# Layer 0's products of probabilities with v: fp32 products replaced by split fp32r products with hi and lo of v side by side

## The chip, the core and the metric

The kernel runs on one core of a Trainium2 chip. The metric is the device time of one execution in microseconds, the median of several runs. A core has a matrix engine (TensorE, PE in the profile; its weight loads are PEld), VectorE (DVE), ScalarE (ACT), GpSimd (POOL) and SyncE (SP), which work at the same time, each through its own queue of instructions in a fixed order, and wait for one another by semaphores. SBUF is the memory on the chip with 128 partitions, PSUM the banks in which TensorE's products add up.

## The reference, cut to what matters

Two layers of a trunk run for 128 prompt tokens and 512 latent tokens with 1024 features. Layer 0 has two attention mixers beside each other, whose outputs meet in one output projection; then an MLP; layer 1 has another mixer and MLP, which the change doesn't touch.

```python
q_a, k_a, v_a, q_b, k_b, v_b = parts          # of h @ w_in, heads of 64 features
# mixer A: 8 query heads on 2 key and value heads, 512 + 128 (cached) keys, softmax over all 640
s = jnp.einsum('bqkgd,bskd->bkgqs', qi, k).astype(jnp.float32) * scale
p = jax.nn.softmax(s, axis=-1).astype(v.dtype)
o = jnp.einsum('bkgqs,bskd->bqkgd', p, v)
# mixer B: 8 heads; each query reads 8 x 16 neighbours on the grid, with a bias, and 128 cached keys
s = jnp.concatenate([s_loc.reshape(B, H, GRID_W, n_loc), s_ctx], axis=-1)
p = jax.nn.softmax(s, axis=-1).astype(v.dtype)
o = (jnp.einsum('bhqrw,brqwhd->bqhd', p_loc, vn) + jnp.einsum('bhqp,bphd->bqhd', p_ctx, v_ctx))
```

Prompt tokens read only prompt tokens (128 x 128 per head) in both mixers. The new keys and values of the prompt are outputs too.

## The kernel before

Nearly all products of weights with activations are split: a value x is kept as hi = fp32r(x) and lo = x - hi, both in fp32r (fp32 numbers that TensorE reads with less precision), and three products hi·hi, lo·hi and hi·lo add up in one bank (L245 to L247 for blocks of 128 features and 320 tokens, L463 to L465 for 256 columns token by token). The products of probabilities with v aren't split: both sides are fp32.

Layer 0's attention is `attn_layer`. After the modulation and norm come mixer A's q, k and v, their norms and the rotary step (`ev_kv` puts v's blocks into `va`, feature rows `qaT` hold the queries, `kha` the split keys). Then `pair_a` runs for four pairs of heads. For each head and 128 queries the scores (L691) lie in PSUM, VectorE takes their maximum (L616), ScalarE the exponential with sums (L621), VectorE the sums' reciprocals (L622), GpSimd multiplies (L623). `turned` transposes four blocks of 128 x 128 probabilities into one bank `t` (L631), and one copy brings them to SBUF as `pt`: by VectorE for the odd head of a pair (L634), by ScalarE for the even one (L636). The product with v (L700) takes 64 columns of v as stationary side and 512 queries as moving side, for five key blocks. The two heads of a pair write to the upper and the lower 64 partitions of one bank `o`; five products each add up, and VectorE copies the bank to a tile `oa` (L704). `prompt_block` does the same for the prompt's 128 x 128 (L645 to L658).

Behind the pairs in the program's order stand `pieces`, the projections of mixer B's v (evacuated to `vall` by ScalarE, L710), q and k (`ev_b`, L722 to L743: copy, square, sum over partitions by a product, logarithm and exponential, multiply). The scheduler places them among the heads' instructions, wherever TensorE would wait. Then mixer A's outputs `oa` are split into hi and lo (L235 on ScalarE, L236 on VectorE).

Mixer B's pool of buffers takes the place of mixer A's queries, keys and v (`mid`). The cached keys of all heads come in one load `craw` (L769, on ScalarE's queue), and become `ckb`, hi and lo (L770, L771). `front(h)` is a head's scores (L797 to L801), the bias add (L803) with a bias block from HBM (L781, SyncE's queue), and softmax. Hi and lo of the head's keys `kk` are made by L783 and L784 and sent to the other 64 partitions by a DMA (L786). `back(pr, pss)` does the products with v of two heads side by side in one bank: the 128 cached keys for all 512 queries (L823), then four key blocks for 256 queries each (L833). `put_b` splits the bank straight from PSUM: hi on ScalarE (L813), lo on VectorE (L814). The order of the fronts, prompt blocks and backs is a list: F0 F1 F2 F3 P0 P1 B0 F4 F5 P2 B1 F6 F7 P3 B2 B3. Filling work in mixer B are products of modulation weights (L170).

This whole part stands in one phase that a scheduler orders by a timeline of its own; the order of each engine's instructions is fixed when the program is built. The phase ends with a barrier of all engines (L78).

## Time and profile before

| what | us |
| --- | --- |
| median of 3 runs | 1877.26 |
| the runs | 1877.03, 1877.26, 1878.83 |
| span of the profiled execution, first to last instruction | 1874.1 |
| layer 0's attention with its norm, start to the barrier L78 | 0 to 358 |
| mixer A's heads with mixer B's projections | 95 to 282 |
| mixer B's heads | 282 to 358 |

The profile is of one execution on the one core; its own device time outside the span isn't listed apart. Times in rows are microseconds from the span's start. A window gives how long each engine was busy in a stretch; a group of instructions gives busy time, mean ns of one, and the idle time in front of them with what ended it; a row of a timeline gives start, duration, engine, line, operation, output and inputs. An fp32 product appears as two records. A matmul's record is longer than the distance between two starts, since matmuls are pipelined: costs of TensorE are read from the starts. In a shape such as 128\*64 the second number is that of the stationary columns.

### The profile page before, as it was taken

To read this page: it belongs to the slowest core of one execution; us is meant where nothing else is said; L and a number is where in the kernel's file an instruction comes from. 1 tells how busy PE (TensorE), PEld (TensorE's weight loads), DVE (VectorE), ACT (ScalarE), POOL (GpSimd) and SP (SyncE) were. 2 spreads that over 40 slices of the span, in tenths; PEclk is the share of its full clock that TensorE was granted. 3 is DMA by queue.
4 is the path that set the end of the run, shared out by engine and by line. 5 is a ranking of instruction groups with operands and counts; after the bars stand their busy time and mean duration, and the time that the engine had idled before them with its cause. 6 is when DMAs were issued, how large, how long until landed. Compare 5 with 4: busy or idle time off the path is not lost.

```text
span 1874.1 us, 34901 instructions
## 1 busy us (share of the span) xinstructions
PE 1792.9 (96%) x14416; PEld 1662.4 (89%) x14416; DVE 1120.3 (60%) x2252; ACT 781.6 (42%) x1725; POOL 252.3 (13%) x252
## 2 busy tenths in 40 slices
PE   5899998999999999999989999999999999999999
PEld 4887776698999999999888878888999999999999
DVE  5745348478766666746687877776447434343342
ACT  4535456345223131233655656655635213132230
POOL 1223314211000000001332222222111000000000
PEclk9999999999999999999999999999999999999999
DMA  9201028524454344423223122232132222222221
GB/s 317 77 27 48 25 81 289 181 75 157 138 177 135 136 146 147 158 97 103 72 53 74 48 47 69 48 89 74 49 124 77 82 68 75 83 68 72 87 75 50
DMA packets 174990, 187.21 MB, mean 100 GB/s; under 512 B 48456, under 2 KB 152136, under 8 KB 174832
## 3 DMA queue, kind: packets, MB, share of 16 engines
q1 hardware_dynamic: 170272, 175.05, 29.7%
q0 software_dynamic: 1408, 5.41, 0.9%
q10 hardware_dynamic: 3152, 4.52, 0.7%
q8 instruction: 113, 1.85, 0.4%
q14 instruction: 45, 0.37, 0.1%
HBM read 170.97 MB, written 11.37 MB: 97 GB/s over the span
## 4 chain that ended last, share of the span: by engine, by line
PE 59%; DVE 10%; issue 7%; ACT 3%; DMA 1%; POOL 1%; DVEq 0%; SPq 0%; POOLq 0%; ACTq 0%
PE dn L245 10%; PE dn L246 9%; PE dn L247 9%; PE p L245 8%; PE p L246 8%; PE p L247 8%; DVE t L229 1%; DMA t<-in_w_out_dram 1%; PE p L1265 1%; PE p L1256 1%; PE ob L1258 1%; PE ob L1282 1%; DVE at L1116 1%; PE p L1277 1%; PE s L1046 1%
## 5 line engine op out<-in xcount | busy, mean ns | idle before, releaser
L228 ACT CAST t<-t 128x1024 fp32r<-128x1024 f32 x157 | 164.4, 1048 | 346.3 <-PE p L246 237.8
L245 PE MATMUL dn<-t 128*128 128x320 f32 x936 | 298.7, 319 | 4.1 <-PEq L78 3.1
L246 PE MATMUL dn<-t 128*128 128x320 f32 x936 | 299.3, 320 | 1.3 <-DVE t L395 0.8
L247 PE MATMUL dn<-t 128*128 128x320 f32 x936 | 297.6, 318 | 0.0
L229 DVE TENSOR_TENSOR t<-t 128x1024 fp32r<-128x1024 f32 x157 | 193.4, 1233 | 121.7 <-ACT t L228 121.3
L245 PEld LDWEIGHTS dn<-t 128*128 128x128 f32 x936 | 178.1, 190 | 9.6 <-issue 5.4
L246 PEld LDWEIGHTS dn<-t 128*128 128x128 f32 x936 | 178.0, 190 | 6.0 <-issue 2.5
L247 PEld LDWEIGHTS dn<-t 128*128 128x128 f32 x936 | 178.0, 190 | 3.3 <-issue 2.5
L245 PE MATMUL p<-t 128*128 128x320 f32 x488 | 152.0, 311 | 0.0
L247 PE MATMUL p<-t 128*128 128x320 f32 x488 | 151.6, 311 | 0.0
L246 PE MATMUL p<-t 128*128 128x320 f32 x488 | 151.6, 311 | 0.0
L407 DVE SCALAR_TENSOR_TENSOR x<-p,t,x 128x192 f32<-128x192 f32 (+2 forms) x154 | 53.3, 386 | 143.6 <-PE p L247 143.6
L246 PE MATMUL p<-hl,t 128*128 128x320 f32 x448 | 138.4, 309 | 0.0
L192 DVE SCALAR_TENSOR_TENSOR ma<-t,ma 128x1024 f32<-128x1024 f32 x98 | 123.4, 1280 | 18.7 <-DMA t<-in_mod_w_dram 18.7
L246 PE MATMUL dn<-hl,t 128*128 128x320 f32 x416 | 128.5, 309 | 0.0
L245 PE MATMUL p<-hh,t 128*128 128x320 f32 x392 | 121.1, 309 | 0.0
L247 PE MATMUL p<-hh,t 128*128 128x320 f32 x392 | 121.1, 309 | 0.0
L245 PE MATMUL dn<-hh,t 128*128 128x320 f32 x376 | 116.4, 310 | 0.0
L247 PE MATMUL dn<-hh,t 128*128 128x320 f32 x376 | 116.2, 309 | 0.0
L429 ACT CAST hh<-h 128x320 fp32r<-128x320 f32 x128 | 58.7, 459 | 126.9 <-DVE h L428 126.9
L388 POOL TENSOR_TENSOR nt<-x,rs 128x320 f32<-128x320 f32 x30 | 31.4, 1062 | 566.6 <-ACT rs L308 536.9
L246 PEld LDWEIGHTS p<-t 128*128 128x128 f32 x488 | 92.3, 189 | 0.2
(458 smaller groups left out, 4575.6 us busy)
## 6 DMA issues: line engine op xcount, KB each, us to landing
t<-in_mlp_w_dram SPq DMA_DIRECT2D x64, 1024.0 KB
t<-in_mod_w_dram SPq DMA_DIRECT2D x40, 1024.0 KB, 7.0
t<-in_w_qkv_dram SPq DMA_DIRECT2D x12, 1024.0 KB
t<-in_w_in_dram SPq DMA_DIRECT2D x9, 1024.0 KB, 5.9
w<-in_mod_w_dram SPq DMA_DIRECT2D x4, 2048.0 KB, 16.4
t<-in_w_out_dram SPq DMA_DIRECT2D x8, 1024.0 KB, 5.2
bias<-in_biasx_dram SPq DMA_DIRECT2D x8, 512.0 KB, 6.8
t<-in_w_z_dram SPq DMA_DIRECT2D x4, 1024.0 KB
```

The source lines that it names most:

```text
L192: nc.vector.scalar_tensor_tensor(out=acc[v], in0=wt[:, k], scalar=c, in1=acc[v], op0=ALU.mult, op1=ALU.add)
L228: nc.scalar.copy(hi, raw)
L229: nc.vector.tensor_tensor(out=lo, in0=raw, in1=hi.bitcast(F32), op=ALU.subtract)
L245: self.nc.tensor.matmul(ps, lhsT=hi[:, k, :], rhs=xh[:, ts_], start=(k == 0), stop=False)
L246: self.nc.tensor.matmul(ps, lhsT=hi[:, k, :], rhs=xl[:, ts_], start=False, stop=False)
L247: self.nc.tensor.matmul(ps, lhsT=lo[:, k, :], rhs=xh[:, ts_], start=False, stop=(k == NK - 1))
L388: nc.gpsimd.tensor_tensor(out=t, in0=xt[k][:, c], in1=rs[:, c], op=ALU.mult)
L407: nc.vector.scalar_tensor_tensor(out=xout[:, a:b], in0=ps[:, a - o:b - o], scalar=self.mod_vec(layer, idx, k, v), in1=xin[:, a:b], op0=ALU ...
L429: nc.scalar.copy(hh[:, ts_], h)
L1046: nc.tensor.matmul(pn[32 * g:32 * g + 32, 0:3 * P], lhsT=n.ones[:, 0:32], rhs=sq[g % 2][:, g // 2 * 2 * P:g // 2 * 2 * P + 3 * P], start=T ...
L1116: nc.vector.scalar_tensor_tensor(out=aa[:, d, b0 + b, :], in0=ps[:, b, 0], scalar=bk[:, b0 + b, d:d + 1], in1=ga[d][:, b0 + b, :], op0=ALU ...
L1256: nc.tensor.matmul(p1s[d][:, 0:128], lhsT=K[:, 0, bs], rhs=S[d], start=True, stop=True)
```

## The change

`split_v` keeps v in fp32r as 128 columns for each head: 64 of hi and 64 of lo (`va`, `vall`); every evacuation of v becomes a cast by ScalarE and a subtraction by VectorE, and so do the cached v, which now come by way of a tile `cv`. The prompt's new v for the output is copied apart (`vo`). `turned` makes hi (ScalarE) and lo (VectorE) of each transposed bank, in 2 + 2 buffers in place of 4, for every head. `with_v` is the product: one with all 128 columns (v's hi and lo) and hi of the probabilities, whose output has 128 partitions, and one with the 64 columns of v's hi and lo of the probabilities into the first 64 partitions. `halves` adds the bank's two halves: ScalarE copies the lower one to SBUF, VectorE adds. Each head now has the bank `o` to itself, and the heads of a pair come one after the other in both mixers. Mixer A's result is written over its queries `qaT`, and their split stands ahead of the release of mixer A's pool. Mixer B's result goes to a tile `ob` and is split from there.

```diff
+    def split_v(dst, src):
+        sv = src.rearrange("p (h d) -> p h d", d=HD)
+        nc.scalar.copy(dst[:, :, 0:HD], sv)
+        nc.vector.tensor_tensor(out=dst[:, :, HD:2 * HD], in0=sv, in1=dst[:, :, 0:HD].bitcast(F32), op=ALU.subtract)
...
-        vall = qp.tile([P, 6, HB * HD], F32, name="vall")
+        vall = qp.tile([P, 6, HB, 2 * HD], F32R, name="vall")
-        va = [ap_.tile([P, KVA * HD], F32, name=f"va{blk}") for blk in range(6)]
+        va = [ap_.tile([P, KVA, 2 * HD], F32R, name=f"va{blk}") for blk in range(6)]
...
-            p = n.wsp.tile([P, nb * w], F32, tag=f"p{nb}", name="p", bufs=8 if nb == 1 else 10)
+            p = n.wsp.tile([P, nb * w], F32, tag=f"p{nb}", name="p", bufs=7 if nb == 1 else 10)
...
-            pt = n.wsp.tile([P, 512], F32, tag="pt", name="pt", bufs=4)
-            if j:
-                nc.vector.tensor_copy(pt[:, 0:w], t[:, 0:w])
-            else:
-                nc.scalar.copy(pt[:, 0:w], t[:, 0:w])
-            return pt
+            hi, lo = (n.wsp.tile([P, 512], F32R, tag=f"pt{i}", name="pt", bufs=2)[:, 0:w] for i in range(2))
+            mulsub(hi, lo, t[:, 0:w])
+            return hi, lo
+
+        def with_v(out, v, hi, lo, start, stop):
+            nc.tensor.matmul(out, lhsT=v, rhs=hi, start=start, stop=False, skip_group_check=True)
+            nc.tensor.matmul(out[0:HD], lhsT=v[:, 0:HD], rhs=lo, start=False, stop=stop, skip_group_check=True)
+
+        def halves(dst, o):
+            w = o.shape[1]
+            u = n.wsp.tile([P, 512], F32, tag="oh", name="oh", bufs=1)
+            nc.scalar.copy(u[HD:P, 0:w], o[HD:P])
+            nc.vector.tensor_tensor(out=dst, in0=o[0:HD], in1=u[HD:P, 0:w], op=ALU.add)
...
-                    pts = [turned(j, [pb[:, 0, kb * P:(kb + 1) * P] for pb in pss[j]]) for j in range(2)]
-                    for j in range(2):
-                        nc.tensor.matmul(o[64 * j:64 * j + 64, :], lhsT=vs[kb if kb < 4 else 5], rhs=pts[j], start=(kb == 0), stop=(kb == 4))
+                heads = [qaT[pr][64 * j:64 * j + 64] for j in range(2)]
+                for j in range(2):
+                    o = n.bank("o")
+                    for kb in range(5):
+                        pt = turned([pb[:, 0, kb * P:(kb + 1) * P] for pb in pss[j]])
+                        with_v(o, vs[kb if kb < 4 else 5], *pt, kb == 0, kb == 4)
+                    halves(heads[j][:, 0:TS], o)
...
-                sq = bp.tile([P, T], F32, tag="bsq", name="bsq")
+                sq = bp.tile([P, T], F32, tag="bsq", name="bsq", bufs=1)
...
+        for k, t in enumerate(qaT):
+            n.split_act(k, t)
         mid.close()
-        for k, t in enumerate(oT):
-            n.split_act(k, t)
...
+                oT = out_b(TS, 1)
                 for j in range(2):
-                    nc.tensor.matmul(o[64 * j:64 * j + 64, :], lhsT=val(5, j), rhs=pts[j], start=True, stop=False, skip_group_check=True)
...
+                    o = n.bank("o")
+                    with_v(o, val(5), *turned([pb[:, 256:384] for pb in pss[j]]), True, False)
...
+                            with_v(ov, val(kb), *(x[:, ji * 256:(ji + 1) * 256] for x in pt), False, kb == 3)
+                    halves(oT[64 * j:64 * j + 64], o)
+                split_b(pr, oT, [(0, 384, 64), (384, 448, 0), (448, 512, 448)])
```

Comments are gone from the changed file, so lines move: L691 becomes L707, L803 L817, L769 L783; the helper of hi and lo (before L450, L451) is L445 and L446, and `turned` and `put_b`'s splits now go through it.

How the instructions stand on the queues is shown at three places. The names are the tiles' (`t` is also that of transposes' banks, of weights and of split activations), the last number is the output's shape, and in brackets are the engines or DMA queues that an instruction waits for. First TensorE, around mixer A's first products with v; before:

```order
L700 MATMUL o<-pt,va_536 64x512 [waits Activation_85]
L631 MATMUL t<-t,p 128x128 [waits PE_85]
L631 MATMUL t<-t,p 128x128 x3
L463 MATMUL dn<-t 128x256
L464 MATMUL dn<-t 128x256
L465 MATMUL dn<-t 128x256
L700 MATMUL o<-pt,va_536 64x512 [waits DVE_85]
L631 MATMUL t<-t,p 128x128 [waits PE_85]
L631 MATMUL t<-t,p 128x128 x3
L700 MATMUL o<-pt,va_537 64x512 [waits Activation_85]
L631 MATMUL t<-t,p 128x128 [waits PE_85]
```

and after:

```order
L645 MATMUL o<-pt,va_536 64x512 [waits DVE_85]
L637 MATMUL t<-t,p 128x128 [waits PE_85]
L637 MATMUL t<-t,p 128x128
L644 MATMUL o<-pt,va_537 128x512 [waits Activation_85]
L637 MATMUL t<-t,p 128x128 x2
L465 MATMUL dn<-t 128x256
L466 MATMUL dn<-t 128x256
L645 MATMUL o<-pt,va_537 64x512 [waits DVE_85]
L660 MATMUL t<-kha_544,qs 128x128 [waits PE_85]
```

A product is now two, the second of which waits for VectorE's lo, and other work stands between the two or behind them; transposes for the other head of the pair no longer alternate with these.

Second ScalarE, where mixer B begins: the load of the cached keys and what stands around it (`bx` and `bsq` are the evacuation and norm of a projection of mixer B, `qs` the split queries). Before:

```order
L769 DMA craw<-in_ctxk_dram 128x1024 [waits DVE_85,PE_85]
L450 CAST qs<-qbT_523 64x640 x2
L450 CAST qs<-qbT_524 64x640 x2
L734 ACTIVATE bsq<-t 128x320 [waits PE_85]
L734 ACTIVATE bsq<-dn,t 128x320 [waits PE_85]
L783 CAST t<-kbT_527 64x640 [waits PE_85]
L734 ACTIVATE bsq<-o,t 128x320 [waits PE_85]
L735 ACTIVATE bsq<-bsq 128x640 [waits Activation_85]
L734 ACTIVATE bsq<-dn,t 128x320 [waits PE_85]
L770 CAST ckb_2859<-craw 128x1024 [waits DMAHW2_85]
```

and after:

```order
L749 ACTIVATE bsq<-o,t 128x320 [waits PE_85]
L737 COPY bx<-sc 128x320 [waits PE_85]
L750 ACTIVATE bsq<-bsq 128x640 [waits Activation_85]
L783 DMA craw<-in_ctxk_dram 128x1024 [waits DMAHW0_85,DVE_85]
L445 CAST qs<-qbT_523 64x640 x2
L445 CAST qs<-qbT_524 64x640
L797 CAST kk_3051<-kbT_528 64x640
L445 CAST qs<-qbT_524 64x640
L744 ACTIVATE bsq<-bx 128x640 [waits DVE_85]
L784 CAST ckb_3056<-craw 128x1024 [waits DMAHW0_85]
```

The load waited for TensorE's and VectorE's use of mixer A's buffers, with projections still to come; now it waits for VectorE's splits of mixer A's output and stands behind the evacuation of the last projection.

Third VectorE, at the end of mixer B, up to the barrier. Before:

```order
L229 TENSOR_TENSOR t<-t 128x1024 [waits Activation_85]
L634 COPY pt<-t 128x512 [waits DVE_85,PE_85]
L814 TENSOR_TENSOR t<-o,t 128x384 [waits Activation_85]
L634 COPY pt<-t 128x512 [waits DVE_85,PE_85]
L814 TENSOR_TENSOR t<-o,t 128x64 [waits Activation_85] x2
L634 COPY pt<-t 128x512 [waits DVE_85,PE_85]
L814 TENSOR_TENSOR t<-o,t 128x384 [waits Activation_85]
L814 TENSOR_TENSOR t<-o,t 128x64 [waits Activation_85] x2
```

and after:

```order
L446 TENSOR_TENSOR t<-ob,t 128x384 [waits Activation_85]
L446 TENSOR_TENSOR t<-ob,t 128x64 [waits Activation_85] x2
L446 TENSOR_TENSOR pt<-t,pt 128x512 [waits PE_85,Activation_85]
L446 TENSOR_TENSOR pt<-t,pt 128x512 [waits Activation_85]
L652 TENSOR_TENSOR ob<-o,oh 64x512 [waits DVE_85,Activation_85]
L446 TENSOR_TENSOR pt<-t,pt 128x512 [waits Activation_85]
L446 TENSOR_TENSOR pt<-t,pt 128x512 [waits PE_85,Activation_85]
L652 TENSOR_TENSOR ob<-o,oh 64x512 [waits Activation_85]
L446 TENSOR_TENSOR t<-ob,t 128x384 [waits Activation_85]
L446 TENSOR_TENSOR t<-ob,t 128x64 [waits Activation_85] x2
```

Each bank of transposes passes over VectorE, and each head has an add of its halves (L652) ahead of the split.

## Rows read from the trace of the kernel before

**Rows 1.** The profile page's span, and its section 1.

```profile
span 1874.1 us, 34901 instructions
...
PE 1792.9 (96%) x14416; PEld 1662.4 (89%) x14416; DVE 1120.3 (60%) x2252; ACT 781.6 (42%) x1725; POOL 252.3 (13%) x252
```

**Rows 2.** Windows: busy us by engine (instructions), granted clock, DMA share, GB/s.

```profile
70.00:80.00 10.00, 10.00 (x86) 10.00 (x85) 10.00 (x23) 5.45 (x16) 4.09 (x6) 1.00 0.36 109
95.00:256.00 161.00, 159.80 (x984) 120.77 (x984) 72.62 (x126) 68.06 (x150) 47.20 (x36) 0.99 0.10 30
282.00:300.00 18.00, 12.94 (x132) 9.56 (x131) 16.65 (x31) 13.97 (x40) 6.17 (x8) 1.00 0.91 290
300.00:340.00 40.00, 39.72 (x329) 26.62 (x330) 30.30 (x61) 22.89 (x72) 16.68 (x16) 0.96 0.77 253
282.00:358.00 76.00, 66.81 (x566) 44.45 (x565) 56.53 (x110) 45.50 (x131) 25.74 (x24) 0.98 0.66 217
```

**Rows 3.** Groups by line and shape, 95 to 256 us (mixer A).

```profile
L700 PE MATMUL o<-pt,va 128*64 128x512 f32 x80 | 39.7, 618 | 0.1
...
L634 DVE COPY pt<-t 128x512 f32<-128x512 f32 x20 | 13.8, 691 | 47.2 <-PE t L631 47.1
...
L636 ACT COPY pt<-t 128x512 f32<-128x512 f32 x20 | 11.7, 587 | 33.1 <-PE t L631 33.1
```

**Rows 4.** Timeline of TensorE in mixer A: start us, us, instruction.

```profile
155.56 0.27 PE L631 MATMUL t<-t,p 128*128 128x128 f32 x1
155.76 1.07 PE L700 MATMUL o<-pt,va 128*64 128x512 f32 x2
156.77 0.41 PE L245 MATMUL dn<-t 128*128 128x320 f32 x1
157.02 0.31 PE L246 MATMUL dn<-t 128*128 128x320 f32 x1
157.16 0.31 PE L247 MATMUL dn<-t 128*128 128x320 f32 x1
```

**Rows 5.** Timeline around mixer B's start, all engines; last, the DMA issues.

```profile
255.26 0.36 ACTq L769 DMA_DIRECT2D craw<-in_ctxk_dram  x1
...
255.66 2.98 ACT L450 CAST qs<-qbT 64x640 fp32r<-64x640 f32 x4 [1.85 <-PE o L658]
...
262.13 1.03 ACT L770 CAST ckb<-craw 128x1024 fp32r<-128x1024 f32 x1
...
263.19 1.23 DVE L771 TENSOR_TENSOR ckb<-craw,ckb 128x1024 fp32r<-128x1024 f32 x1 [0.86 <-ACT ckb L770]
...
282.12 0.31 PE L247 MATMUL sc<-t 128*128 128x320 f32 x1
...
282.32 0.74 ACT L735 ACTIVATE bsq<-bsq 128x640 f32<-128x640 f32 x1
...
283.32 0.70 DVE L803 TENSOR_TENSOR sc<-sc,bias 128x512 f32<-128x512 f32 x1
...
craw<-in_ctxk_dram ACTq DMA_DIRECT2D x1, 512.0 KB, 6.5
```

**Rows 6.** Groups by line and shape, 282 to 358 us (mixer B).

```profile
L833 PE MATMUL o<-pt,vall 128*64 128x256 f32 x64 | 11.0, 391 | 0.4 <-ACT pt L636 0.4
...
L823 PE MATMUL o<-pt,vall 128*64 128x512 f32 x16 | 5.4, 618 | 0.0
```

**Rows 7.** Timeline of VectorE and TensorE at the end of mixer B.

```profile
338.38 0.70 DVE L803 TENSOR_TENSOR sc<-sc,bias 128x512 f32<-128x512 f32 x1 [0.20 <-PE sc L801]
...
357.25 0.23 DVE L814 TENSOR_TENSOR t<-o,t 128x64 fp32r<-128x64 f32 x1 [0.28 <-ACT t L813]
...
352.38 1.08 PE L823 MATMUL o<-pt,vall 128*64 128x512 f32 x4
353.29 2.07 PE L833 MATMUL o<-pt,vall 128*64 128x256 f32 x16
358.42 0.38 PE L245 MATMUL dn<-t 128*128 128x320 f32 x1 [3.06 <-PEq L78]
```

More of the change, by code (lines that the diff above doesn't have):

```diff
@@ L440, in attn_layer @@
     I, O = n.i, n.o
[L441 to L446 removed]
+    bps = ExitStack()
     def mulsub(hi, lo, src):
@@ L806, in front, with out_b @@
                 return pbs, q, kk
-            def put_b(pr):
-                def put(ps, pieces):
-                    hi, lo = n.act[8 + 2 * pr:10 + 2 * pr]
-                    for a, b, d in pieces:
-                        c = slice(d, d + b - a)
-                        nc.scalar.copy(hi[:, c], ps[:, a:b])
-                        nc.vector.tensor_tensor(out=lo[:, c], in0=ps[:, a:b], in1=hi[:, c].bitcast(F32), op=ALU.subtract)
-                return put
+            def out_b(w, bufs):
+                return wp.tile([P, w], F32, tag=f"ob{w}", name="ob", bufs=bufs)
```

78 lines of the change are left out of this document (36 added, 42 removed).

## The prediction

> **What bounds the kernel now.** I read the page first, then the windows, then lines, single rows and waits of the stretches that the change touches. The span is 1874.1 us and TensorE is busy for 96% of it [rows 1]. The change lies in layer 0's attention, the first 358 us; the next part starts behind a barrier, at 358.42, where TensorE's idle time is put down to its own sequencer [rows 7]. The instructions behind that barrier stand in the same order as before, so I let those 1516 us stay as they are. What matters is when the barrier is reached.
>
> The windows [rows 2] show four stretches with different limits. At 70 to 80 us (norms and rotary step of mixer A) VectorE is busy for 10.00 of 10 us. From 95 to 256 us (mixer A's heads, with projections as filling) TensorE is busy for 159.80 of 161 us and VectorE for 73: TensorE's own time counts. From 282 to 300 us (mixer B begins) TensorE has 12.94 of 18, VectorE 16.65: VectorE leads. From 300 to 340 us TensorE has 39.72 of 40 and VectorE 30.30: both are well filled. Behind 340 a chain of transposes, copies and products runs out, from the last bias add at 338.38 to the last subtraction at 357.25 [rows 7]. A gain in the second stretch can so be given back in the three others.
>
> **Mixer A, products with v.** A lone product starts at 155.76 and the next work at 156.77: 1.01 us [rows 4]. The 80 records of the 40 products [rows 3] have starts that add up to 37.1 us, 0.93 each, since some follow one another. The first wide product behind takes 0.25 us (156.77 to 157.02), the second 0.15 (157.02 to 157.16) [rows 4]: going from 64 stationary columns back to 128 costs 0.10 in that row. With a somewhat longer last record I take 0.15 for a change of shape. The 40 products cost 37.1 us and 0.14 each for what lies outside, 42.7 us.
>
> Now each is a product of 128 and one of 64 stationary columns, 512 moving columns, fp32r. No row has an fp32r product with 64. The nearest is the fp32r product with 128: 0.15 us for 320 columns [rows 4], 0.23 for 512; a quarter of the fp32 product, as if it were four passes, is 0.23 also. I take 0.22. Going to 64 columns and back costs two changes: 0.22 + 0.22 + 0.30 = 0.74 us, times 40 is 29.6 us, **13.1 us less**. The ends: no cost for a change, 17.6 us and 25 less; the 64-column product at the old 0.93, 58 us and 15 more. I stay at 0.74 since fp32r and the change both have near rows. Four prompt blocks get 16 short products for 8, with changes of shape: 1.7 us more (estimate, 0.2 us a product). So TensorE's time in this stretch falls by 11.4 us.
>
> The Trainium skill, "TensorEngine Tiling (Array Packing)", Theoretical Speedup and Key Properties, says that up to 64 columns leave room for two tiles that work in parallel, up to twice as fast; that speaks against the change. The trace shows it where two heads' products adjoin, in mixer B: four records, two products, in 0.91 us (352.38 to 353.29) [rows 7]. In mixer A 1.01 us for a lone product says that it was hardly used. Had it been, the 40 products would have cost some 24 us, the change would save nothing here, and the time would be about 1900 us.
>
> **What the copies become.** Every transposed block had one copy, 0.59 us on ScalarE or 0.69 on VectorE, 20 each in this stretch [rows 3]. Now each of the 40 has both, one behind the other: 20 more on each engine, 11.7 and 13.8 us. The new sum of the halves adds a copy and an add per head (0.59 and 0.69), the splits of v more short ones. VectorE goes from 73 to about 90 us and ScalarE from 68 to about 87, of some 150: TensorE hides them, if filling stands between a transpose and its product. With two banks for transposes, two buffers each for hi and lo, and one bank for a head's sum, I add 1.5 us of new waits (0 to 4; 40 blocks with 0.1 us each uncovered is 4). The eight copies of mixer A's output go away; they were hidden and bring nothing.
>
> **Ahead of mixer A** VectorE is full [rows 2], and five splits of v's blocks and the cache's come there: six subtractions at 0.3 us (between 0.23 for 64 columns [rows 7] and 0.69 for 512 [rows 3]), **1.8 us more** (0 to 3). So the last projection ends 11.4 - 1.5 - 1.8 = **8.1 us earlier** than 282.12 (4 to 12).
>
> **Mixer B's start.** Before, the load of the cached keys was issued at 255.26 on ScalarE's queue, its cast ran at 262.13 and its subtraction at 263.19, all under the projections; the first bias add came at 283.32, 1.2 us behind the last projection's start at 282.12 [rows 5]. Now this buffer lies where mixer A's queries lie, and these become free only when mixer A's output in them has been split. Those splits write over the projections' input, so they can't end before the last projection. On ScalarE's queue the load now stands behind the copy of the last projection and an exponential of 0.74 us [rows 5]: issued some 1.3 us behind the last projection. It lands 6.5 us later [rows 5]; the casts of queries queued meanwhile (2.98 us for four) lie under that. Then cast 1.03, subtraction 1.23, and about 1 us of scores: the first bias add comes 1.3 + 6.5 + 1.03 + 1.23 + 1 = 11 us behind the last projection, 10 more than before. SyncE's queue has the first bias block behind the splits too, which lands in the same time. What TensorE, VectorE and ScalarE do meanwhile (modulation products, prompt scores, key splits) they did later before; I count 2 us as given back: **8 us more** (5 to 10).
>
> **The rest of mixer B.** VectorE gets 12 more blocks of 512 at 0.69, two or so of 256, eight adds of 512 columns and eight of 128: 8.3 + 0.8 + 5.5 + 2 = some 15 us on top of 56.5 [rows 2]; ScalarE about the same on 45.5. TensorE: two heads' products took 3.0 us in one go (352.38 to 355.36) [rows 7], but the 80 records [rows 6] lie scattered, and with changes of shape and prompt products I count 21.8 us before. Now a head has five pairs: 512 columns 0.44, four of 256 at 0.24, five times 0.30: 2.9 us, eight heads 23.2, prompts about 4: **5 us more** (1.5, without cost for a change less than nothing, to 11). TensorE's 66.8 us become 72, VectorE's 56.5 become 71.5. The stretch is 76 us. If VectorE is filled as at 282 to 300, 93%, it needs 77; at its mean of 74% it needs 96. TensorE alone needs 72. I take the middle, 83%: 86 us, **10 us more** (2 to 20). More than half of that I expect behind the last bias add, where heads that were done side by side come one after the other, each with copy, subtraction, products, copy, add, and the second waits for the first one's bank.
>
> **Sum.** -8.1 + 8 + 10 = +10 us. The profiled span is 1874.1 us, the median of the runs 1877.26; that execution's time outside its span isn't listed, and I take the 3.2 us between them as unchanged. So 1877.3 + 10 = **1887 us**.
>
> **Rivals.**
> 1. *Mixer B takes its new work in its gaps, and mixer A's gain stays.* TensorE is idle for 9 of 76 us there, VectorE for 19, and the wait at the start would be filled with work that came later. Decides if the start and the rest together cost under 4.4 us, since 8.1 are gained: start 3, rest 1, TensorE's gain at its 12 end: 1877 - 12 + 4 = 1869, or 1873 with the middle gain. For it: the row of 282 to 358 leaves room. Against it: VectorE at 93% in the first 18 us, and a tail in which each step waits for the one before.
> 2. *Gain and loss cancel*: gain 8 to 12, start 5, rest 4: 1877 us. It needs both losses at their low ends.
> 3. *The 64-column fp32r product isn't faster than the old one*, so the change doesn't do what it says: 0.93 + 0.22 + 0.30 for each of 40, 58 us; 28 us more than in the sum, and some 15 more in mixer B: about 1925 us. No row has it, but the 128-column row speaks against it.
>
> **How the numbers follow.** Forecast, slower, 1887 us: 0.60. Rival 1: 0.22. Rival 2: 0.15. Rival 3: 0.03. The measurement can tell a change of about 0.2%, 3.75 us: faster 0.22, same 0.15, slower 0.63. Where it is slower, 1881 to 1903 holds most. Over all cases 8 in 10 lie from 1870 (half of rival 1) to 1902 us (mixer B at its upper end, +18, with the other terms in the middle, and rival 3 left out).
>
> **What would show it.** Right: lines of mixer A's two new products with starts about 0.3 us apart and the window's TensorE time some 11 us smaller; the last projection 4 to 12 us earlier; the load of cached keys behind it and the first bias add 8 to 11 us behind it; over 20 us between the last bias add and the barrier. Wrong: if the 64-column product takes over 0.5 us, if the first bias add follows the projections within 4 us, or if mixer B's stretch is not longer than 78 us. Changes behind the barrier would mean that I missed a part.

## The result: 12.5 us slower

The changed kernel takes 1889.8 us (median of 4 runs, 1885.53 to 1891.11) beside 1877.35 us for the kernel before: 1.0058 times as long, 95% interval 1.0042 to 1.0073. The forecast was 1887 us, range 1870 to 1902, slower 0.63.

The page of the changed kernel, its span and its section 1, answers [rows 1]:

```profile
span 1889.4 us, 35114 instructions
...
PE 1786.3 (95%) x14416; PEld 1686.4 (89%) x14416; DVE 1160.7 (61%) x2329; ACT 816.9 (43%) x1798; POOL 250.7 (13%) x252
```

TensorE is busy for 6.6 us less, VectorE for 40 more, ScalarE for 35 more, and the span is 15.3 us longer. The time was thus not lost in TensorE's work. The windows say where. The columns are those of [rows 2]; the borders are the changed kernel's own: norms of mixer A, mixer A, last projection to first bias add, start, middle and end of mixer B.

```profile
70.00:80.00 10.00, 10.00 (x86) 10.00 (x85) 10.00 (x22) 5.68 (x15) 3.96 (x6) 1.00 0.37 111
95.00:267.20 172.20, 163.13 (x1123) 148.95 (x1122) 100.48 (x175) 101.19 (x217) 45.92 (x36) 0.99 0.13 38
267.20:277.50 10.30, 7.25 (x57) 5.09 (x57) 8.45 (x11) 8.21 (x13) 5.15 (x8) 0.83 0.91 303
277.50:300.00 22.50, 15.05 (x113) 10.33 (x116) 12.98 (x24) 10.14 (x31) 4.92 (x7) 0.62 0.89 272
300.00:343.80 43.80, 35.53 (x286) 28.36 (x279) 37.66 (x74) 29.28 (x82) 17.18 (x16) 0.84 0.69 209
343.80:371.20 27.40, 19.51 (x117) 14.26 (x115) 19.81 (x41) 16.95 (x41) 2.93 (x2) 0.94 0.00 1
```

The last projection starts at 267.17 in place of 282.12, **14.95 us earlier**. Behind it mixer B takes 104.1 us (to 371.24, the end of the last subtraction) in place of 75.4 (282.12 to 357.48 [rows 5, 7]), **28.7 us more**. In the second window TensorE is busy for 95% of the time; from 277.5 to 300 it has 15.05 of 22.5 us at a granted clock of 0.62, where [rows 2] have 1.00. The barrier is reached 13.8 us later, and what lies behind it takes 1518.2 us in place of 1516.6.

Mixer B is best cut in three: from the last projection to the third bias add (the second head's first; a head's scores fill both of the tiles `sc`, so the third bias add waits until the first two exponentials have read the first one), from there to the last bias add, and the end behind that. Before, the cuts are 282.12, 289.52, 338.38 and 357.48; now 267.17, 293.00, 343.76 and 371.24. This gives 7.4, 48.9 and 19.1 us before, and 25.8, 50.8 and 27.5 after. **The middle, where most of the new copies are, costs 1.9 us; the start costs 18.4 and the end 8.4.**

*The start.* ScalarE of the changed kernel: start us, us, instruction, idle time before it and what ended it.

```profile
267.58 0.36 ACTq L783 DMA_DIRECT2D craw<-in_ctxk_dram  x1
...
279.60 0.35 ACTq L758 DMA_DIRECT2D out_new_k_dram<-ko  x1
281.39 0.37 ACT L150 COPY modm<-dn 128x256 f32<-128x256 f32 x1 [1.82 <-PE dn L170]
288.39 0.58 ACT L627 ACTIVATE p<-sc,nm 128x384 f32<-128x384 f32 x1 [6.63 <-DMA t<-t]
```

VectorE in the same stretch:

```profile
273.78 1.22 DVE L785 TENSOR_TENSOR ckb<-craw,ckb 128x1024 fp32r<-128x1024 f32 x1
...
277.54 1.29 DVE L817 TENSOR_TENSOR sc<-sc,bias 128x512 f32<-128x512 f32 x2
...
279.47 0.94 DVE L622 TENSOR_REDUCE nm<-sc 128x2 f32<-128x768 f32 x1
...
289.66 0.17 DVE L628 RECIPROCAL smx<-smx 128x2 f32<-128x2 f32 x1 [7.13 <-ACT p L627]
...
293.00 0.69 DVE L817 TENSOR_TENSOR sc<-sc,bias 128x512 f32<-128x512 f32 x1
```

The load of the cached keys is issued behind the last projection, not before it as in [rows 5], and the first bias add comes at 277.54, 10.4 us behind 267.17. But then there is a second, larger hole: the first exponential runs only at 288.39. VectorE's maximum, which it needs, was there at 280.41 (279.47 + 0.94), so it is not that which it waits for. The row names a transfer that ended at that time; the experiments below show which it is.

TensorE in that hole and behind it:

```profile
276.83 0.33 PE L811 MATMUL sc<-t,qs 128*128 128x256 f32 x1
277.00 0.33 PE L815 MATMUL sc<-ckb,qs 128*128 128x128 f32 x2
...
288.23 1.93 PE L170 MATMUL dn<-t 128*32 128x256 f32 x16 [5.98 <-DMA t<-in_mod_w_dram]
...
290.58 0.52 PE L811 MATMUL sc<-t,qs 128*128 128x256 f32 x1
290.90 0.31 PE L815 MATMUL sc<-ckb,qs 128*128 128x128 f32 x1
```

After 6 us of waiting for a modulation load, the same 256-column product takes 0.32 us (290.58 to 290.90) that took 0.17 at 276.83 (to 277.00): the granted clock from 288 to 293 us is 0.50, its lower level, 1.2 GHz.

*The end.* The last bias add, and VectorE's adds of the last two heads' halves:

```profile
343.76 0.68 DVE L817 TENSOR_TENSOR sc<-sc,bias 128x512 f32<-128x512 f32 x1
...
365.30 0.68 DVE L652 TENSOR_TENSOR ob<-o,oh 64x512 f32<-64x512 f32 x1 [0.21 <-ACT oh L651]
...
369.15 0.69 DVE L652 TENSOR_TENSOR ob<-o,oh 64x512 f32<-64x512 f32 x1 [1.27 <-ACT oh L651]
```

And TensorE's first product of a head: of the fourth head, of the fifth, and of the last two:

```profile
345.31 0.50 PE L644 MATMUL o<-pt,vall 128*128 128x512 f32 x1 [0.57 <-DVE ob L652]
...
354.07 0.74 PE L644 MATMUL o<-pt,vall 128*128 128x512 f32 x1
...
362.02 0.50 PE L644 MATMUL o<-pt,vall 128*128 128x512 f32 x1
...
366.04 0.50 PE L644 MATMUL o<-pt,vall 128*128 128x512 f32 x1 [0.23 <-DVE ob L652]
```

A head takes 4.0 us here (354.07 to 366.04 for three), and the last one's products start 0.06 us behind the add that frees the one bank (365.30 + 0.68 = 365.98). But a head took no less before. The products of the last two pairs, in the kernel before:

```profile
344.37 1.08 PE L823 MATMUL o<-pt,vall 128*64 128x512 f32 x4
...
352.38 1.08 PE L823 MATMUL o<-pt,vall 128*64 128x512 f32 x4
```

They start 8.0 us apart, 4.0 for a head. The 8.4 us come at the two borders of this stretch. At its start a fifth head stands behind the last bias add (345.31), and the last four heads begin 10.3 us behind it (343.76 to 354.07) in place of 6.0 (338.38 to 344.37). At its end the last pair's two heads, which before ended 5.1 us behind their first product (352.38 to 357.48), now take 9.2 one after the other (362.02 to 371.24). The late begin makes 4.3 us of the 8.4, the last pair 4.1.

### The profile page after: what moved, and what is told of

It reads as the page before. It is cut to its first block, busy times and chain, and to the rows that moved or that the text cites. A ratio compares the mean times of both kernels' runs of the same rounds, so it can differ in the third digit from the quotient of the medians.

```text
span 1889.4 us, 35114 instructions
## 1 busy us (share of the span) xinstructions
PE 1786.3 (95%) x14416; PEld 1686.4 (89%) x14416; DVE 1160.7 (61%) x2329; ACT 816.9 (43%) x1798; POOL 250.7 (13%) x252
## 4 chain that ended last, share of the span: by engine, by line
PE 57%; DVE 11%; issue 7%; ACT 3%; DMA 2%; POOL 1%; DVEq 0%; SPq 0%; POOLq 0%; ACTq 0%
PE dn L245 9%; PE dn L246 9%; PE dn L247 9%; PE p L246 7%; PE p L245 7%; PE p L247 7%; DVE t L229 1%; DMA t<-in_w_out_dram 1%; PE p L1269 1%; PE p L1278 1%; PE ob L1271 1%; PE ob L1295 1%; DVE ma L192 1%; DVE at L1129 1%; PE p L1290 1%
## 5 line engine op out<-in xcount | busy, mean ns | idle before, releaser
L388 POOL TENSOR_TENSOR nt<-x,rs 128x320 f32<-128x320 f32 x30 | 31.1, 1051 | 567.7 <-ACT rs L308 538.0
```

The lines of the kernel that those rows point to most:

```text
L388: nc.gpsimd.tensor_tensor(out=t, in0=xt[k][:, c], in1=rs[:, c], op=ALU.mult)
```

## The experiments

Medians and stages of all kernels, in us. "To 3rd add", "middle" and "end" are the three parts of mixer B; "over before" and the ratio are to the kernel before as it ran beside them on the same chip (medians 1876.69 to 1878.23), and differences between kernels are taken from that column.

| kernel | median | over before | ratio (95%) | last projection | to 3rd add | middle | end |
| --- | --- | --- | --- | --- | --- | --- | --- |
| before | 1877.35 | 0 | 1 | 282.1 | 7.4 | 48.9 | 19.1 |
| after | 1889.80 | +12.5 | 1.0058 (1.0042 to 1.0073) | 267.2 | 25.8 | 50.8 | 27.5 |
| lo128 | 1897.87 | +21.2 | 1.0113 (1.0094 to 1.0131) | 266.6 | 29.8 | 48.4 | 34.1 |
| a_only | 1861.13 | -15.6 | 0.9918 (0.9903 to 0.9932) | 261.5 | 6.8 | 52.7 | 20.1 |
| b_only | 1918.71 | +42.0 | 1.0220 (1.0205 to 1.0236) | 292.0 | 26.7 | 48.9 | 33.7 |
| after_aq | 1893.33 | +16.6 | 1.0087 (1.0069 to 1.0105) | 271.0 | 26.3 | 48.4 | 30.7 |
| mem | 1885.81 | +7.6 | 1.0036 (1.0023 to 1.0050) | 279.0 | 22.0 | 46.9 | 17.5 |
| aq_ko | 1885.14 | +6.9 | 1.0041 (1.0029 to 1.0053) | 268.3 | 18.0 | 51.2 | 27.6 |
| aq_ko_nohalves | 1890.31 | +12.1 | 1.0067 (1.0052 to 1.0083) | 268.6 | 15.4 | 52.2 | 38.1 |
| byhead | 1887.59 | +10.6 | 1.0051 (1.0034 to 1.0068) | 285.5 | 7.4 | 49.9 | 31.3 |
| hi_only | 1873.03 | -4.0 | 0.9982 (0.9972 to 0.9993) | 270.0 | 15.6 | 52.1 | 23.8 |
| warm | 1882.99 | +6.0 | 1.0035 (1.0021 to 1.0049) | 268.5 | 15.4 | 54.3 | 29.6 |

Stages are those of one profiled execution each. `byhead` has the instructions of the kernel before, in the same order, up to mixer B's products with v, and its last projection starts at 285.5 in place of 282.1: by some 3 us such a stage can differ without a cause in the code, and 2 us in one stage say little.

**What the 64-column product costs.** In `lo128` the product with lo of the probabilities has all 128 columns too, so TensorE never changes its shape between the two:

```diff
-            nc.tensor.matmul(out[0:HD], lhsT=v[:, 0:HD], rhs=lo, start=False, stop=stop, skip_group_check=True)
+            nc.tensor.matmul(out, lhsT=v, rhs=lo, start=False, stop=stop, skip_group_check=True)
```

> The changed kernel, but the second product of each pair takes all 128 columns (hi and lo of v) instead of 64, so that the shape of the array never changes between the two. Theory S (as in the prediction, a change of shape costs 0.15 us): some 0.3 us less for each of 96 pairs, of which mixer A's 48 lie on TensorE's path: last projection 8 to 14 us earlier than 267.2, time 1877-1883. Theory N (the rows of the changed kernel show 0.23 us from a 64-column product to the next 128-column one, so the change costs nothing): last projection within 2 us of 267.2, time 1887-1892.

The last projection starts at 266.64, within 0.6 us of 267.17: mixer A gains nothing from the one shape. TensorE's timeline of this kernel in mixer A:

```profile
151.19 0.39 PE L645 MATMUL o<-pt,va 128*128 128x512 f32 x1
151.43 0.39 PE L644 MATMUL o<-pt,va 128*128 128x512 f32 x1
151.66 0.40 PE L645 MATMUL o<-pt,va 128*128 128x512 f32 x1
```

And of the changed kernel, with both shapes:

```profile
165.44 0.39 PE L644 MATMUL o<-pt,va 128*128 128x512 f32 x1
165.68 0.40 PE L645 MATMUL o<-pt,va 128*64 128x512 f32 x1
165.91 0.39 PE L644 MATMUL o<-pt,va 128*128 128x512 f32 x1
166.14 0.39 PE L645 MATMUL o<-pt,va 128*64 128x512 f32 x1
166.37 0.60 PE L637 MATMUL t<-t,p 128*128 128x128 f32 x4
```

All starts lie 0.23 to 0.24 us apart in both. A 64-column product with 512 moving columns is as long as a 128-column one, and the change from one to the other costs nothing that these rows show. The Trainium skill, "TensorEngine Tiling (Array Packing)", Key Properties, says that a change of tiling mode drains TensorE; between these two fp32r shapes the trace has no such cost beside the 0.23 us. The whole kernel is 8.7 us slower than the changed one and above both theories' times, with 29.8 us to the third bias add in place of 25.8 and an end of 34.1 in place of 27.5. In the end the copy of the halves has to wait for the second product too, which I take for the reason there; no run separates it.

**Which half of the change costs what.** `a_only` splits v and the probabilities in mixer A alone and leaves mixer B and `vall` as they were before; mixer A's output stays in tiles of its own, so the cached keys are loaded as early as before:

```diff
-        va = [ap_.tile([P, KVA * HD], F32, name=f"va{blk}") for blk in range(6)]
+        va = [ap_.tile([P, KVA, 2 * HD], F32R, name=f"va{blk}") for blk in range(6)]
...
+                for j in range(2):
+                    o = n.bank("o")
+                    for kb in range(5):
+                        pt = turned_split([pb[:, 0, kb * P:(kb + 1) * P] for pb in pss[j]])
+                        with_v(o, vs[kb if kb < 4 else 5], *pt, kb == 0, kb == 4)
+                    halves(heads[j][:, 0:TS], o)
...
-                sq = bp.tile([P, T], F32, tag="bsq", name="bsq")
+                sq = bp.tile([P, T], F32, tag="bsq", name="bsq", bufs=1)
```

> Mixer A alone changed (split products, head by head, output in tiles of its own as before), mixer B as before. Theory 1 (mixer A's gain is real and reaches the end if mixer B isn't touched): the last projection ends 13 to 16 us earlier than 282.1, mixer B keeps its 75 us, time 1861-1865. Theory 2 (mixer B can't start earlier, since its loads and key splits then run late): the gain shrinks to under 6 us, 1871-1877.

It takes 1861.13 us, 15.6 us less than the kernel before and 28 less than the changed one: the fastest of all. Its windows (mixer A; last projection to the end of mixer B):

```profile
95.00:261.53 166.53, 157.28 (x1110) 143.97 (x1110) 98.28 (x168) 101.18 (x215) 51.93 (x44) 1.00 0.18 57
261.53:341.20 79.67, 70.44 (x548) 46.74 (x546) 58.52 (x110) 46.41 (x133) 25.61 (x24) 0.94 0.62 195
```

Mixer A ends 20.6 us earlier, more than the 13 to 16 expected, and mixer B gives back 4.3 of it.

`b_only` is `after_aq` (below) with mixer A's products in fp32 again:

```diff
-        va = [ap_.tile([P, KVA, 2 * HD], F32R, name=f"va{blk}") for blk in range(6)]
+        va = [ap_.tile([P, KVA * HD], F32, name=f"va{blk}") for blk in range(6)]
...
+                    pts = [turned_f(j, [pb[:, 0, kb * P:(kb + 1) * P] for pb in pss[j]]) for j in range(2)]
+                    for j in range(2):
+                        nc.tensor.matmul(o[64 * j:64 * j + 64, :], lhsT=vs[kb if kb < 4 else 5], rhs=pts[j], start=(kb == 0), stop=(kb == 4))
```

> Mixer B alone changed (split products head by head), mixer A's products fp32 and side by side as before, queries in a pool of their own so that mixer B's start isn't late. Theory 1 (mixer B loses by itself: halves, splits, one bank per head in turn): the last projection stays at 281 to 284 us, mixer B takes 84 to 90 us instead of 75, time 1887-1893. Theory 2 (mixer B's loss in the changed kernel comes only from its late start): 1876-1881.

1918.71 us: mixer B's half of the change alone costs 42 us, some 25 more than either theory allowed. Mixer B takes 109.3 us, and the last projection comes 9.9 us later than before though mixer A's products are the old ones. From the first score of mixer A to it are 191.9 us in place of 184.4; what is new in that stretch is the splits of `vall`'s blocks, which hold the projections' one bank for a cast and a subtraction (in the changed kernel VectorE waits 5.1 us there for the cast). That these splits are the 7.5 us is argued, not shown. But the same price shows a second time: with mixer A's products split, the last projection starts at 261.5 without mixer B's half (`a_only`) and at 271.0 with it (`after_aq`, below), 9.5 us later; with the old products it is 282.1 and 292.0, 9.9 us. And mixer A's products gain 20.6 and 21.0 us in these two comparisons. The whole kernels don't add up like that: -15.6 and +42.0 make +26.4, and `after_aq` has +16.6.

**Is it the late load of the cached keys?** `after_aq` gives mixer A's queries a pool of their own, so the buffer for the cached keys doesn't wait for the last split of mixer A:

```diff
-        qaT = [ap_.tile([P, T], F32, name=f"qaT{p}") for p in range(4)]
+        aqs = ExitStack()
+        aq = aqs.enter_context(tc.tile_pool(name="aq", bufs=1, side="right"))
+        qaT = [aq.tile([P, T], F32, name=f"qaT{p}") for p in range(4)]
```

> The changed kernel, but mixer A's queries (over which its output is written) lie in a pool of their own, so that mixer B's first buffers, cached keys among them, no longer wait for the splits of mixer A's output. Theory 1 (the late start of mixer B is a loss of its own, and the burst of loads and the half clock behind it come from it): the load of the cached keys goes out over 5 us before the last projection, the first bias add comes within 3 us behind the last projection instead of 10.4, and the time falls by 9 to 15 us to 1875-1881. Theory 2 (mixer B is bound by its own new copies, so that an earlier start only lengthens later waits): the first bias add is earlier but the last is not, time 1886-1890.

The first bias add comes 1.2 us behind the last projection, as before the change; but the third comes 26.3 us behind it (changed kernel: 25.8), and the whole is 4.2 us above the changed kernel, above both theories' times. The early start is lost in the same later wait. Two of its waits from 271 to 300 us (what waited, for what; us in total, times, longest):

```profile
PE dn L170 <- DMA t<-in_mod_w_dram: 8.5, 4, 5.3
ACT p L629 <- DMA out_new_k_dram<-ko: 7.4, 1, 7.4
```

The first exponential waits for the store of `ko`, a tile of the projections which neither it nor its inputs use. Its output `p` does not lie on `ko` either: in the program `p`'s first buffer is far below it. But `p` comes from the same pool as `pt`, `pp` and `oh`, and the exponential is the first to write to this pool. In the changed kernel the pool ends at byte 228,864 of each partition, and the projections' pool, whose last tile is `ko`, begins at 219,104; before, the two lay 6 KB apart. `vall` with twice the columns takes 12 KB of the difference; without them the pools would lie 2.5 KB apart. So the pool's first writer waits for the last reader of everything that it lies on. The transfers that the program has the exponential wait for are stores alone: in the changed kernel, in `after_aq` and in `mem` (below) the last one of `ko` and older ones, in `aq_ko` (below) only an old one of mixer A.

**Is it the room alone?** `mem` is the kernel before, with a `vall` of twice the size whose second half nobody uses (and mixer A's queries and output in one pool, for want of room):

```diff
-        vall = qp.tile([P, 6, HB * HD], F32, name="vall")
+        vall = qp.tile([P, 6, 2 * HB * HD], F32, name="vall")
```

> The kernel before, with its products as they were, but the tile of mixer B's v twice as large (the second half unused), as the split v makes it, and mixer A's output written over its queries in a pool of their own. So only the room that is left changes, and mixer B's buffers of probabilities come to lie where ko was. Theory 1 (room alone costs): the first exponential waits over 4 us for the transfer of the new keys, time 1882-1890. Theory 2 (room alone costs nothing): 1875-1880.

1885.81 us, 1.0036 times the kernel before: **7.6 us for room, without one product or copy more**. The queries' pool has a part in it: it moves the projections' tiles 10 KB down, so that mixer B's pool would reach their first ones, though not `ko`, without the larger `vall` too. The third bias add comes 22.0 us behind the last projection in place of 7.4; middle and end are 3.6 us shorter than before. ScalarE of this kernel:

```profile
289.19 0.34 ACTq L745 DMA_DIRECT2D out_new_k_dram<-ko  x1
292.01 0.37 ACT L150 COPY modm<-dn 128x256 f32<-128x256 f32 x1 [2.85 <-PE dn L170]
296.45 0.58 ACT L623 ACTIVATE p<-sc,nm 128x384 f32<-128x384 f32 x1 [4.07 <-DMA t<-in_mod_w_dram]
```

As in the changed kernel the first exponential runs behind the store of `ko`: 7.3 us after its issue here, 7.4 in `after_aq`, 8.8 in the changed kernel (279.60 to 288.39). Here, as there, the row names another transfer that ended near that time: such a name is a guess by time. The time that the store takes from issue to landing (the last number, in us) settles it, in the changed kernel (first) and in `mem` (second):

```profile
out_new_k_dram<-ko ACTq DMA_DIRECT2D x1, 64.0 KB, 8.7
```

```profile
out_new_k_dram<-ko ACTq DMA_DIRECT2D x1, 64.0 KB, 7.2
```

It lands at 288.3 and at 296.4, and the exponential starts some 0.1 us behind it in both.

`aq_ko` is `after_aq` with `ko` in another pool, and one `p` buffer fewer to make room:

```diff
-            p = n.wsp.tile([P, nb * w], F32, tag=f"p{nb}", name="p", bufs=7 if nb == 1 else 10)
+            p = n.wsp.tile([P, nb * w], F32, tag=f"p{nb}", name="p", bufs=7 if nb == 1 else 9)
...
-                    ko = bp.tile([P, P], F32, tag="ko", name="ko")
+                    ko = qp.tile([P, P], F32, tag="ko", name="ko", bufs=2)
```

> The changed kernel with mixer A's queries in a pool of their own (as after_aq), and with the tile ko, from which the prompt's new keys go to HBM, in a place that mixer B's buffers never take (for room, mixer B has 9 buffers of probabilities instead of 10). In after_aq the first exponential of mixer B waited 7.4 us for that transfer, with the other engines idle and the clock at half behind it. Theory 1 (this one wait, and the clock that falls with it, are most of mixer B's loss beyond the forecast): no such wait, TensorE's clock at 2.4 GHz to 300 us, mixer B 10 to 18 us shorter, time 1874-1883. Theory 2 (mixer B's chain of copies by itself): the wait goes and 2 to 6 us with it, time 1886-1892.

1885.14 us, 6.9 over the kernel before where `after_aq` has 16.6: the wait for the store is worth 9.7 us by the medians, 8.3 up to the third bias add. Its time lies between those of the two theories. What is left, from the same view at 268 to 290 us:

```profile
ACT p L629 <- DVE kbT L754: 1.4, 1, 1.4
```

The first exponential still waits for VectorE's last read of the projections' tile `bx` (line 754), the end of the whole norm of the last projection, where before it stood ahead of that norm's last squares and roots. Mixer B's pool still lies on `bx`. So the third bias add still comes 18.0 us behind the last projection, not 7.4.

**Do the new products, copies and adds of mixer B cost the rest?** Two kernels take work out of `aq_ko`. `aq_ko_nohalves` leaves out lo of v in mixer B, with it the copy and the add of the halves; each head is split straight from its bank:

```diff
+        def first(out, v, hi, lo, start, stop):
+            nc.tensor.matmul(out[0:HD], lhsT=v[:, 0:HD], rhs=hi, start=start, stop=False, skip_group_check=True)
+            nc.tensor.matmul(out[0:HD], lhsT=v[:, 0:HD], rhs=lo, start=False, stop=stop, skip_group_check=True)
...
-                    halves(oT[64 * j:64 * j + 64], o)
-                split_b(pr, oT, [(0, 384, 64), (384, 448, 0), (448, 512, 448)])
+                    split_h(pr, j, o, [(0, 384, 64), (384, 448, 0), (448, 512, 448)])
```

> As aq_ko, but in mixer B's products over the window the columns of v's lo are left out: both products have the 64 columns of v's hi, nothing is to be added from the other half, and the result is split straight from PSUM, head by head (so the output lacks lo of v there). Against aq_ko: theory 1 (the halves' copy and add, 1.3 us a head in a chain of which every head waits, are the larger part of what mixer B got): 7 to 12 us less than aq_ko. Theory 2 (the transposes' two copies in a row are): 0 to 4 us less.

It takes 1890.31 us, 5 more than `aq_ko` where both theories had less. The end grows from 27.6 to 38.1 us: three casts and three subtractions hold each head's bank where one copy and one add held it, and the last four heads' products start 5.1 us apart (354.57 to 369.80 for three) in place of 3.9. So the run doesn't price the copy and the add, since it put something longer in their place; it shows that the time for which a head holds the one bank counts in the end.

`hi_only` leaves out lo of the probabilities in mixer B, with it the second copy of each transposed bank and the 64-column products:

```diff
+            if j:
+                nc.vector.tensor_copy(hi, t)
+            else:
+                nc.scalar.copy(hi, t)
...
-                    with_v(o, val(5), *turned([pb[:, 256:384] for pb in pss[j]]), True, False)
+                    with_hi(o, val(5), turned_hi(0, [pb[:, 256:384] for pb in pss[j]]), True, False)
```

> As aq_ko, but in mixer B's products over the window lo of the probabilities is left out (the output lacks it): one copy per bank of transposes, by ScalarE and VectorE in turn, and one product of 128 columns instead of two. The halves, the room and the order by head stay. Theory 1 (the second copy of each bank, behind the first, is what lengthens mixer B): 10 to 16 us less than aq_ko, 1869-1875. Theory 2 (the order by head and the one bank): 2 to 6 us less, 1879-1883.

1873.03 us, 10.9 less than `aq_ko` over the kernel before, as the first theory had it: the second copies and the 64-column products of mixer B are worth more than all that `aq_ko` loses. The profiled execution of it (1876.95 us) is near the slowest of its ten, and shows 5 of the 11: mixer B 91.6 us in place of 96.7, with the start 2.3 and the end 3.8 us shorter, the middle 1.0 longer. In the middle the doubled copies of the transposed banks are hidden in this trace. In the end they are not: the last four heads' products start 2.9 us apart (349.10 to 357.84 for three) in place of 3.9. For the rest there is no trace.

**Is it the order of the heads?** `byhead` is the kernel before, fp32 with one copy for a transposed bank, but in mixer B each head has the bank to itself, one head after the other, and is split from it:

```diff
-                    pts = [turned(j, [pss[j][b][:, f * P:(f + 1) * P] for b, f in use]) for j in range(2)]
...
+                    o = n.bank("o")[r]
+                    pt = turned(0, [pb[:, 256:384] for pb in pss[j]])
...
+                        pt = turned(1 - jj, [pss[j][b][:, f * P:(f + 1) * P] for b, f in use])
```

> The kernel before, with mixer B's products with v still fp32 and unsplit, but head by head: each head has the bank to itself, its three banks of transposes are copied in turn by ScalarE, VectorE, ScalarE, and its result is split from PSUM before the next head's products begin. Only the order of the heads changes, no product and no copy of transposes is added (the split of the result is in twice as many pieces). Theory 1 (that heads no longer run side by side is a large part of mixer B's 21 us): mixer B 8 to 15 us longer, 1885-1893. Theory 2 (the added copies are, the order isn't): 0 to 4 us, 1877-1881.

1887.59 us, 1.0051 times the kernel before, with no product more. Its windows (mixer B; the end of it) and the row of VectorE that ends each of the last heads' long split:

```profile
285.52:374.05 88.53, 74.46 (x566) 48.71 (x564) 59.92 (x118) 51.79 (x147) 25.72 (x24) 0.96 0.59 186
342.79:374.05 31.26, 23.59 (x138) 12.92 (x133) 14.99 (x34) 14.52 (x39) 2.93 (x2) 1.00 0.11 34
```

```profile
357.44 0.55 DVE L835 TENSOR_TENSOR t<-o,t 64x384 fp32r<-64x384 f32 x1 [1.54 <-ACT t L834]
...
362.40 0.56 DVE L835 TENSOR_TENSOR t<-o,t 64x384 fp32r<-64x384 f32 x1 [1.54 <-ACT t L834]
...
367.51 0.55 DVE L835 TENSOR_TENSOR t<-o,t 64x384 fp32r<-64x384 f32 x1 [1.54 <-ACT t L834]
```

Start and middle are those of the kernel before, within 1 us. The end is 31.3 us in place of 19.1, at a granted clock of 1.00: about 5.0 us for each head, and no engine is full (TensorE, the busiest, 23.59 of 31.26 us). One head after another in one bank makes the end longer by 12.2 us, part of it by the six short splits for a pair in place of three, which hold the bank. A pair side by side took 8.0 us before, two heads take 10 here; and here too a fifth head stands behind the last bias add. The changed kernel, with its copy and add, loses 8.4 there.

**Is it TensorE's clock?** In mixer B the mean granted clock is 0.98 before and 0.82 after the change. `warm` is `aq_ko` with each transposed bank of mixer B written twice, the same values in the same place, to give TensorE more to do:

```diff
-            for i, x in enumerate(pieces):
-                nc.tensor.transpose(out=t[:, i * P:(i + 1) * P], in_=x, identity=n.ident)
+            for _ in range(WARM[0] if len(pieces) == 4 else 1):
+                for i, x in enumerate(pieces):
+                    nc.tensor.transpose(out=t[:, i * P:(i + 1) * P], in_=x, identity=n.ident)
```

> As aq_ko, but in mixer B every bank of four transposes is written twice (the second over the first): 96 more transposes of 0.11 us, 10.5 us more for TensorE, and nothing else. Theory 1 (TensorE's idle time, by which its clock falls to 1.2 GHz for some 25 us of mixer B, costs more than this work): the clock in mixer B rises from 0.87 to over 0.93 and the time stays or falls, 1879-1886. Theory 2 (the added work lies on the chain and the clock is a consequence that costs little): 5 to 11 us more, 1890-1896.

Mixer B of `aq_ko` (first fence) and of `warm` (second), the columns as above:

```profile
268.34:365.07 96.73, 73.11 (x536) 55.52 (x534) 75.06 (x140) 60.36 (x163) 25.78 (x24) 0.87 0.46 149
```

```profile
268.49:367.81 99.32, 81.37 (x632) 65.91 (x630) 74.56 (x140) 61.12 (x163) 26.48 (x24) 0.88 0.48 146
```

TensorE is busy for 8.3 us more, mixer B is 2.6 us longer in the profiled execution, and over the kernel before `warm` has 6.0 us, `aq_ko` 6.9 (the ranges of their runs, 1880.91 to 1890.53 and 1882.49 to 1890.78, overlap). The first theory's time came, but not its reason: the clock rose by 0.01 only, so the run doesn't tell what the lower clock costs; that stays open. It tells that most of the added work lay in TensorE's idle time: its own work isn't what sets mixer B's length.

## Why the prediction was right, and where its steps were not

The sign, the size and the reason in the large hold: mixer A ends earlier and mixer B gives back more. But that the sum came out so near was luck: two terms were wrong in opposite directions. Mixer A was 6.9 us better than forecast (14.95 us lies outside its 4 to 12), mixer B 10.7 worse.

- **Mixer A's products: right sign, too small.** Forecast 0.74 us for a pair and 1.5 us of waits, 31.1 us for 40; the starts of the changed kernel's 80 products add up to 27.3 us, some 4 us of waits among it. The step that failed is the 0.15 us for a change of shape, read from [rows 4]. That row stands behind an fp32 product. Between two fp32r products the change costs nothing (165.44 to 166.37), and `lo128` shows that avoiding it brings nothing. The 0.10 us in [rows 4] belong to the step from fp32 to fp32r, or to the fp32 product itself; which, no run tells. Had the old products in mixer A run two heads side by side, the prediction had some 1900 us by way of no gain there; the 14.95 us and `a_only` speak against it. The Trainium skill's figure that it weighed there ("TensorEngine Tiling (Array Packing)", Theoretical Speedup, up to twice as fast) is thus not what the old products of mixer A had, at 0.93 us each.
- **Ahead of mixer A: +1.8 forecast.** Its first score starts at 97.34 us, before the change at 97.75: nothing was lost. VectorE is as full at 70 to 80 us as in [rows 2]; where the short subtractions found room, no row here shows.
- **The splits of mixer B's v in mixer A's stretch: not priced.** They and what else mixer B's half changes there move the last projection by 9.5 to 9.9 us (`a_only` to `after_aq`, before to `b_only`); the sum had only 1.5 us of waits. In the changed kernel this may be the difference between its 14.95 us and the 20.6 of `a_only`; no run separates it.
- **The copies hidden under mixer A: right.** In the changed kernel's groups of VectorE, 95 to 267 us, the 40 new subtractions that took the place of 20 copies [rows 3] read:

```profile
L446 DVE TENSOR_TENSOR pt<-t,pt 128x512 fp32r<-128x512 f32 x40 | 26.8, 685 | 4.2 <-ACT pt L445 3.6
```

  They are 13 us more of VectorE, and TensorE is busy for 163.13 of 172.2 us all the same.
- **Mixer B's start: right place, wrong price.** Forecast 11 us from the last projection to the first bias add; it is 10.4 (load issued at once, landed 4.3 us later in place of 6.5, subtraction at 273.78, bias add at 277.54). The 8 us charged for it can't be found: `after_aq` takes the delay away and wins nothing, since the next wait ends at the same distance. What was late next was not asked: the exponentials.
- **Room: missing altogether.** I took `vall`'s doubling for a matter of copies. It moves mixer B's pool onto the projections' tiles, so that the first exponential waits for the last norm and the store of `ko`. Room alone costs 7.6 us by the medians (`mem`, the queries' pool included) and 14.6 up to the third bias add, which in the changed kernel is 18.4 us later. This is the step of the prediction that failed most: the sum had no term for where a larger tile pushes the others.
- **The rest of mixer B: the size, half the reason.** Forecast +10, by VectorE's fill and with over half behind the last bias add; measured 1.9 and 8.4. The size by way of the fill is luck: the forecast had 71.5 us of VectorE's work at 83% (its terms add up to 16.6 us more, not 15, so 73), the trace has 79.0 in 104.1 us, 76%, splits of queries and of the cached keys among it that ran before the last projection earlier. The middle took its copies with 1.9 us. The end got 8.4 us longer, as forecast by heads one after another in one bank, which `byhead` shows without any new copy or product: but a head's 4.0 us are those of before, and the loss lies in a fifth head behind the last bias add and in the last pair. By the medians the second copies and 64-column products are worth 10.9 us (`hi_only` beside `aq_ko`) and the order 10.6 (`byhead` beside the kernel before); what share each has in the changed kernel stays open.
- **The sum.** Forecast -8.1 + 8 + 10 = +10 at the barrier; measured -14.95 + 18.4 + 1.9 + 8.4 = +13.8, and 1.5 more behind it. The spans differ by 15.3 us, the medians by 12.5: the changed kernel's profiled run, 1891.11, is 1.3 us above its median, and its time outside the span is 1.7 us, where the prediction took 3.2 for the kernel before. By 1.7 that kernel's profiled execution was some 1.5 us shorter than its median.
- **Rivals.** The first (mixer A's gain stays) lost here, but `a_only` shows it whole as soon as mixer B is left alone: 1861 us. The second (gain and loss cancel) falls with the ratio's interval, 1.0042 to 1.0073. The third (a slow 64-column product) fell with the 0.23 us; its terms, 28 and 15 us on 1887, give 1930, not 1925. And the range's upper end, 1902, doesn't follow from the terms named for it: -8.1 + 8 + 18 gives 1895.

## What to carry to other kernels

Price a larger long-lived tile by what it pushes: look up which pool of the next stage then lies on tiles of the stage before, and who reads those last; a store to memory counts as such a reader, and here the pool's first writer waited for it though its own buffer lay elsewhere. Where a change pays in one stage and costs in another, make it in the first alone: here that is the difference between 12.5 us lost and 16 us won. Where heads share one bank, count how long each holds it up to its last read and how many heads stand behind the last independent work: there that time comes once for every head, while two side by side end together.

## What the runs showed of the hardware

An fp32r product with 64 stationary columns and 512 moving ones starts 0.23 us before its successor, the same as with 128, whether the two alternate (165.44 to 166.37 in the changed kernel) or 128 stand throughout (`lo128`). At the lower level of the granted clock, behind TensorE's 6 us of waiting, a 256-column product took 0.32 us in place of 0.17. In `warm`, 8.3 us of extra TensorE work in mixer B moved the mean granted clock from 0.87 to 0.88 only. A 64 KB store issued beside 1 MB loads took 8.7 us to land (changed kernel) and 7.2 (`mem`), and 1.5 in `aq_ko` where it was issued at 284.94.
